# One attention layer on one core: the last step's seven products in another order, two weight sums made a step ahead

## The chip, the core and the metric

The kernel runs on one core of a Trainium2 chip. The metric is the device time of one execution in microseconds (us). A core has TensorE (PE; its weight loads are listed apart as PEld), VectorE (DVE), ScalarE (ACT), GpSimd (POOL) and SyncE (SP), which here issues nearly all DMAs. Each engine works through its own instructions in the order in which they are written into its queue.

## The reference

One layer of neighbourhood attention over a grid of 8 x 64 tokens, 16 heads of 128, D = 2048, all in float32:

```python
h = rms_norm(x, norm_pre)                      # x: 512 x 2048
q, k, v, z = split(h @ w_in, 4)                # w_in: 2048 x 8192
o = neighbourhood_attention(q, k, v, rpb)      # all 8 rows, 16 of the 64 columns
y = (o * silu(z)) @ w_out                      # w_out: 2048 x 2048
return x + rms_norm(y, norm_post)
```

## The kernel before

The program runs through ten steps. Step 0 to 7 compute h @ w_in, 1024 columns each (two heads' q, k, v and z); their attention runs beside the next step. Steps 8 (NSTEP) and 9 (LAST) compute the output product with w_out, 1024 columns each.

Every matmul is in a rounded format, so a float32 product is made of three: an operand is split into hi (a CAST on ACT) and lo = operand - hi (a subtraction on DVE), and hi x hi, hi x lo and lo x hi are summed in PSUM. A weight tile is 128x512, 256 KB, loaded as `raw` (NRAW = 4 buffers, by SP) or into one of eight resident tiles `t0` to `t7` (T[k]). `prep(m)` splits the weight of slot m and stands AHEAD = 2 slots ahead of the slot's matmuls; `at_prep` says which raw load is issued behind which prep, at least six preps ahead. `hi`/`lo` are the split weights; `a{k}_{n}` are the split activations.

Steps 0 and 8 are plain: 32 slots of 12 matmuls (L285). The others multiply 2 x 2 blocks in seven products: `B11`, `B12`, `B21`, `B22` are the blocks of the step's weights, the passes P1 to P7 (p = 0 to 6 in the code) have 8 slots of 6 matmuls (L332) each, and some of them take a sum of blocks as weights: T[k] is loaded with B11, and DVE adds raw blocks to it at L240 (`t<-t,raw`), ahead of the split, or behind it at L255. The products are summed in three PSUM chains, `"XYXYZYZ"[p]`: u9X, u9Y, u9Z are those of step 9, two tiles each. `combine` takes a chain's tiles at the end of a pass (s1, s5, e, c11 are its results); where the next pass goes on in the same tiles, PE waits for that reading. In step 9 the order of passes is LATE, and P2, the last, has its weights as the split tiles `a{k}_2`/`a{k}_3`, made from raw504 to raw511 by `late_prep` beside the passes before; its two halves (s = 0, 1) are computed one after the other.

`finish(n, t)` takes quarter n (512 columns) of row block t of y: a Square with a sum on ACT (L655), the product with the post weight gpost on DVE (L656), and, when a row block has all its sums, the mean (L658 to L661) and the power on POOL (L662). `final` then multiplies, adds the block of x (`xres`; for t = 0 it lies in T) and stores the result (L668, L670). Beside the second half of step 8 DVE also turns o * silu(z) back and splits it into `a{k}_n`, with t0 to t7 and zm as scratch (L64 is the helper for work that is kept in the order of the program).

At the start, twelve warm-up matmuls run while x (blocks of 128x512, scaled by gcol on ACT and split) and the first raws arrive.

## Time and profile before

| | us |
|---|---|
| median of 3 runs (lowest, highest) | 895.38 (894.34, 895.58) |
| the profiled execution | 896.13 |
| its span, first to last instruction | 894.4 |
| PE busy | 877.7 (98%) |
| DVE busy | 733.8 (82%) |
| ACT busy | 560.7 (63%) |
| moved by DMA | 168.65 MB, mean 189 GB/s |

In the profile all times count from the span's start. A row "[1.43 <-DVE e L363]" says that the engine stood idle for 1.43 us before it and that a DVE instruction of line 363, which writes e, ended that. "x4" is a group of instructions without a pause worth a row.

### The profile page before, as it was taken

The numbers are of one execution on the slowest core, as the hardware profiler recorded it, in microseconds if no ns is written. First come the engines' busy times: TensorE is split into PE (matmuls) and PEld (weight loads), VectorE is DVE, ScalarE is ACT, GpSimd is POOL, SyncE is SP. The second block draws the span as 40 slices with busy tenths as digits, with TensorE's granted clock in tenths as the row PEclk, the third lists the DMA queues.
The fourth block names the chain that finished last, engine by engine and source line by source line (L and its number), as shares of the span: only waits on it lengthen the run. The fifth ranks groups of instructions, "written<-read, shape, count | busy, mean of one in ns | idle before, by whom it ended". The sixth has DMA issues, their size and how long they took to land. (4 is left out here: it accounts for less than half of the span.)

```text
span 894.4 us, 13143 instructions
## 1 busy us (share of the span) xinstructions
PE 877.7 (98%) x4184; PEld 729.3 (82%) x4184; DVE 733.8 (82%) x1367; ACT 560.7 (63%) x1093; POOL 21.0 (2%) x42
## 2 busy tenths in 40 slices
PE   9999999999999999999999999999999999999995
PEld 8888888888888888888888888888888788888774
DVE  4567979897988898889878987998799845979987
ACT  7666857585758565856675667566766755555451
POOL 0000000000000000000000000000010100000000
PEclk9999999999999999999999999999999999999998
DMA  8768357646763765377547654774486534447877
GB/s 267 210 178 257 97 173 237 204 121 184 234 192 109 223 216 178 115 224 226 167 121 226 210 174 124 235 211 149 147 271 218 157 100 139 141 141 226 269 231 239
DMA packets 88277, 168.65 MB, mean 189 GB/s; under 512 B 10128, under 2 KB 10128, under 8 KB 88208
## 3 DMA queue, kind: packets, MB, share of 16 engines
q1 hardware_dynamic: 85536, 159.95, 59.4%
...
q10 hardware_dynamic: 432, 0.53, 0.2%
q14 instruction: 37, 0.30, 0.1%
...
## 5 line engine op out<-in xcount | busy, mean ns | idle before, releaser
L247 ACT CAST hi<-t 128x512 fp32r<-128x512 f32 x320 | 196.6, 618 | 132.2 <-DVE lo L248 21.5
L248 DVE TENSOR_TENSOR lo<-t,hi 128x512 fp32r<-128x512 f32 x320 | 217.3, 686 | 33.5 <-ACT hi L247 32.7
L248 DVE TENSOR_TENSOR lo<-raw,hi 128x512 fp32r<-128x512 f32 x184 | 125.9, 688 | 68.6 <-ACT hi L247 46.9
L247 ACT CAST hi<-raw 128x512 fp32r<-128x512 f32 x184 | 113.8, 620 | 99.2 <-PE u L285 24.7
L240 DVE TENSOR_TENSOR t<-t,raw 128x512 f32<-128x512 f32 x200 | 134.0, 686 | 7.5 <-DMA raw<-in_w 6.6
L285 PE MATMUL u<-hi,a 128*128 128x512 f32 x512 | 130.9, 392 | 1.4 <-DVE e L380 1.2
L285 PEld LDWEIGHTS u<-hi,a 128*128 128x128 f32 x512 | 94.9, 188 | 21.5 <-DVE e L380 1.8
L285 PE MATMUL u<-lo,a 128*128 128x512 f32 x256 | 70.8, 389 | 0.0
L285 PEld LDWEIGHTS u<-lo,a 128*128 128x128 f32 x256 | 48.0, 188 | 10.0
L255 DVE TENSOR_TENSOR t<-t,raw 128x512 f32<-128x512 f32 x56 | 37.3, 686 | 7.3 <-DMA raw<-in_w 7.3
L332 PE MATMUL u9Y<-hi,a 128*128 128x512 f32 x96 | 26.6, 393 | 0.5 <-ACT hi L247 0.5
L332 PE MATMUL u1Y<-hi,a 128*128 128x512 f32 x96 | 26.8, 396 | 0.0
L332 PE MATMUL u2Y<-hi,a 128*128 128x512 f32 x96 | 26.8, 396 | 0.0
L332 PE MATMUL u4Y<-hi,a 128*128 128x512 f32 x96 | 26.8, 396 | 0.0
L332 PE MATMUL u3Y<-hi,a 128*128 128x512 f32 x96 | 26.8, 396 | 0.0
L332 PE MATMUL u5Y<-hi,a 128*128 128x512 f32 x96 | 26.8, 396 | 0.0
L332 PE MATMUL u7Y<-hi,a 128*128 128x512 f32 x96 | 26.8, 396 | 0.0
L332 PE MATMUL u6Y<-hi,a 128*128 128x512 f32 x96 | 26.8, 396 | 0.0
L332 PEld LDWEIGHTS u9Y<-hi,a 128*128 128x128 f32 x96 | 17.8, 188 | 5.4 <-ACT hi L247 1.4
L545 POOL DMA_DIRECT2D graw<-zm x14 | 7.8, 554 | 561.7 <-DVE zm L539 561.7
L495 ACT ACTIVATE edge<-edge,nm 128x192 f32<-128x192 f32 x32 | 14.5, 455 | 8.7 <-DVE nm L488 8.7
L332 PEld LDWEIGHTS u4Y<-hi,a 128*128 128x128 f32 x96 | 17.4, 188 | 3.2
...
## 6 DMA issues: line engine op xcount, KB each, us to landing
raw<-in_w SPq DMA_DIRECT2D x392, 256.0 KB, 3.0
t<-in_w SPq DMA_DIRECT2D x128, 256.0 KB, 3.0
...
x<-in_xT SPq DMA_DIRECT2D x16, 256.0 KB, 3.9
graw<-zm POOLq DMA_DIRECT2D x14, 256.0 KB, 3.4
...
xres<-in_x SPq DMA_DIRECT2D x12, 256.0 KB, 4.1
out<-xres SPq DMA_DIRECT2D x10, 256.0 KB, 3.0
```

The source lines that it names most:

```text
L240: nc.vector.tensor_tensor(T[k], T[k], src, ALU.add)
L247: nc.scalar.copy(hi, src)
L248: nc.vector.tensor_tensor(lo, src, hi.bitcast(F32), ALU.subtract)
L255: nc.vector.tensor_tensor(T[k], T[k], src, ALU.add)
L285: nc.tensor.matmul(U[n][j], l, r, start=k == 0 and i == 0, stop=k == KT - 1 and i == 2)
L332: nc.tensor.matmul(U[c][s], l, r, start=p in (0, 1, 4) and k == 0 and n == 0, stop=k == KH - 1 and n == 2, skip_group_check=True,)
L495: nc.scalar.activation(p, p, AF.Exp, bias=nm[:, i : i + 1], accum_out=sm[:, i : i + 1])
L545: nc.gpsimd.dma_start(graw[h], z_of[h])
```

## The change

LATE becomes P7, P1, P5, P6, P4, P3, P2. P7's weights are B12 + B22: `t<-B12` is now loaded in the second half of step 8 (instead of B11), and DVE adds raw B22 (raw520 to raw527) to it there. P5's are B11 + B12: in the first half of step 8, B12 is loaded into `zw` tiles, raw B11 (raw512 to raw519) is added, the sum is stored to `wsum` in DRAM, and read back into T while P1 runs. P1's B11 is loaded into T while P7 runs. In LAST the chain Z starts at P7, X at P1 (on the PSUM tiles with tag T) and Y at P5; `combine_last` takes the results in the new order. The late activations lie in `a{k}_3` and N2/N3. In the plain step's second half (n = 1) the product with gpost is put off to slots 1 to 7 of LAST. xres is loaded from slot 16 on, every third slot, and finish of key "22" (quarter 3) comes eight slots sooner. At the start raw0 and raw1 are issued by ACT, ACT's table load follows them, hi0 is cast on DVE, and the first four blocks of x are scaled and split in the order of the program. Small tiles (rc, rcy, ms, msy; mx, sm, nm, rs) become slices of one tile.

```diff
-LATE = (0, 1, 3, 4, 6, 5, 2)
+LATE = (6, 0, 1, 3, 4, 5, 2)
...
+    def load_z(k):
+        Z[k] = cp.tile([P, L], F32, tag="zw", name=f"zw{k}", bufs=2)
+        nc.sync.dma_start(Z[k], w[LAST, B12, k])
+
+    def keep_z(k):
+        nc.sync.dma_start(wsum[k], Z.pop(k))
...
-        return step in PLAIN or p not in (0, 6) or step == LAST and p == 6
+        return step in PLAIN or p not in ((0, 1, 6) if step == LAST else (0, 6))
...
+    def sum_prep(m):
+
+        m -= base(NSTEP)
+        return [N + i * KH + (m - c) // 2 for i, c in ((0, 6), (1, 22)) if m in range(c, c + 2 * KH, 2)]
...
-        nc.sync.dma_start(raws[m], src)
+        (nc.scalar if m < 2 else nc.sync).dma_start(raws[m], src)
...
     def prep(m):
+        if m >= N:
+            i, k = divmod(m - N, KH)
+            t = T[k] if i else Z[k]
+            nc.vector.tensor_tensor(t, t, raws.pop(m), ALU.add)
...
-        if not plain and (p in (1, 3, 4) or step == LAST and p == 6):
+        if not plain and p in (1, 3, 4) and (step, p) != (LAST, 1):
...
-            hi, lo = (A(k, o).rearrange("p a b -> p (a b)") for o in (N2, A22))
+            hi, lo = (A(k, o).rearrange("p a b -> p (a b)") for o in (N2, N3))
...
-        nc.scalar.copy(hi, src)
+        if m == 0:
+
+            nc.vector.tensor_copy(hi, src)
+        else:
+            (act if m < 4 else nc.scalar).copy(hi, src)
...
-        elif p == 4:
+        elif p == 4 and step < LAST:
             load_t(step, B12, k)
...
-        elif p == 6 and step + 1 < NSTEP:
-            load_t(step + 1, B11, k)
+        elif p == 6 and (step + 1 < NSTEP or step == LAST):
+            load_t(min(step + 1, LAST), B11, k)
+        elif p == 0 and step == LAST:
+            nc.sync.dma_start(T[k], wsum[k])
...
+    def begins(step, p):
+        return p in (0, 1, 6 if step == LAST else 4)
...
-            if step == LAST and c == "Z":
+            if step == LAST and c == "X":
                 U[c] = [px.tile([P, L], F32, tag="T", name=f"u{step}{c}{s}") for s in range(2)]
...
+    def combine_last(c, u, p):
+
+        if p == 6:
+            c["22"] = pair("s7")
+            for s in range(2):
+                nc.scalar.copy(c["22"][:, s, :], u[s])
+        elif p == 0:
+            c["12"], c["11"] = pair("s1"), pair("c11")
+            for s in range(2):
+                nc.scalar.copy(c["12"][:, s, :], u[s])
+                nc.vector.tensor_tensor(c["22"][:, s, :], u[s], c["22"][:, s, :], ALU.add)
+        elif p == 1:
+            c["21"] = pair("s5")
+            for s in range(2):
+                nc.vector.tensor_tensor(c["21"][:, s, :], u[s], c["12"][:, s, :], ALU.add)
+        else:
+            for key in {3: ("22", "21"), 4: ("21",), 5: ("12",)}[p]:
+                for s in range(2):
+                    nc.vector.tensor_tensor(c[key][:, s, :], u[s], c[key][:, s, :], ALU.subtract)
...
+        if n == 1:
+
+            at(base(LAST) + 1 + 2 * (t ^ 2), lambda: nc.vector.tensor_tensor(y, src, gb[n], ALU.mult))
+            return
         nc.vector.tensor_tensor(y, src, gb[n], ALU.mult)
...
+    for k in range(KH):
+        at(base(NSTEP) + 1 + 2 * k, load_z, k)
+        at(base(NSTEP) + 5 + 2 * k, keep_z, k)
...
-        at(base(LAST) + (KH + 7 * i // 2 if i < KH else 4 * KH + 4 + 2 * q), load_res, t, q)
+        at(base(LAST) + (2 * KH + 3 * i if i < KH else 4 * KH + 4 + 2 * q), load_res, t, q)
...
-            at(base(LAST) + 5 * KH + 1 + 2 * s, lambda n=n, key=key, s=s: finish(n, 2 + s, C[LAST][key][:, s, :]))
+            at(base(LAST) + (7 - n) * KH + 1 + 2 * s, lambda n=n, key=key, s=s: finish(n, 2 + s, C[LAST][key][:, s, :]))
```

What it moves is seen best in the engines' queues. DVE at the end of step 8, before (lo456 is the first weight of LAST; L64 are the rotations and splits, L240 the adds for P5, L656 the products with gpost):

```order
L248 TENSOR_TENSOR lo456_8393<-t0_142,hi456_8392 128x512
L64 TENSOR_TENSOR a7_3_141<-t7_149,a7_3_141 128x2x256
L240 TENSOR_TENSOR t0_142<-t0_142,raw464_8445 128x512
L248 TENSOR_TENSOR lo457_8412<-t1_143,hi457_8411 128x512
L240 TENSOR_TENSOR t1_143<-t1_143,raw465_8459 128x512
L656 TENSOR_TENSOR y1_0_8418<-u8_1_0_8087,gpost0_7953 128x512
L656 TENSOR_TENSOR y1_1_8424<-u8_1_1_8088,gpost0_7953 128x512
L656 TENSOR_TENSOR y1_2_8430<-u8_1_2_8089,gpost0_7953 128x512
```

And now, from three rows behind the split of `a6_3`, the last reader of t6 as scratch (L281 is the split of a weight, L259 the new adds, L65 the helper, L712 the product with gpost):

```order
L65 TENSOR_TENSOR zm15_7816<-t7_147,zm15_7816 128x256
L65 TENSOR_TENSOR t7_147<-t7_147 128x256
L259 TENSOR_TENSOR t6_146<-t6_146,raw526_8369 128x512
L65 TENSOR_TENSOR t7_147<-t7_147,zm15_7816 128x256
L281 TENSOR_TENSOR lo456_8409<-t0_140,hi456_8408 128x512
L65 TENSOR_TENSOR zm15_7816<-zm15_7816,t7_147 128x256
L65 TENSOR_TENSOR a7_3_139<-t7_147,a7_3_139 128x2x256
L281 TENSOR_TENSOR lo457_8432<-t1_141,hi457_8431 128x512
L712 TENSOR_TENSOR y1_0_8439<-u8_1_0_8079,gpost0_7930 128x512
L259 TENSOR_TENSOR t7_147<-t7_147,raw527_8414 128x512
L712 TENSOR_TENSOR y1_1_8444<-u8_1_1_8080,gpost0_7930 128x512
L281 TENSOR_TENSOR lo458_8459<-t2_142,hi458_8458 128x512
```

The adds for P5 are gone; those for P7 stand between the splits, the ones of t6 and t7 a few rows behind the rows that last read these tiles as scratch, and the products with gpost are parted.

DVE where a chain goes over from one pass to the next, before (L363 reads Z between P4 and P7):

```order
L248 TENSOR_TENSOR lo488_8861<-t0_142,hi488_8860 128x512
L248 TENSOR_TENSOR a1_2_116<-raw505_8877,a1_3_117 128x512
L248 TENSOR_TENSOR lo489_8874<-t1_143,hi489_8873 128x512
L363 TENSOR_TENSOR e_9_8765<-u9Z0_8777,e_9_8765 128x512
L363 TENSOR_TENSOR e_9_8765<-u9Z1_8778,e_9_8765 128x512
L248 TENSOR_TENSOR lo490_8893<-t2_144,hi490_8892 128x512
```

And now, between P5 and P6 (L432 reads Y for s5, L269 adds to T):

```order
L281 TENSOR_TENSOR lo481_8742<-t1_141,hi481_8741 128x512
L432 TENSOR_TENSOR s5_8753<-u9Y0_8657,s1_8645 128x512
L432 TENSOR_TENSOR s5_8753<-u9Y1_8658,s1_8645 128x512
L281 TENSOR_TENSOR lo482_8758<-t2_142,hi482_8757 128x512
L269 TENSOR_TENSOR t1_141<-t1_141,raw489_8802 128x512
L269 TENSOR_TENSOR t2_142<-t2_142,raw490_8830 128x512
```

and between P6 and P4 (L436 reads Y for s7 and s5):

```order
L281 TENSOR_TENSOR lo489_8853<-t1_141,hi489_8852 128x512
L436 TENSOR_TENSOR s7_8553<-u9Y0_8657,s7_8553 128x512
L436 TENSOR_TENSOR s7_8553<-u9Y1_8658,s7_8553 128x512
L436 TENSOR_TENSOR s5_8753<-u9Y0_8657,s5_8753 128x512
L436 TENSOR_TENSOR s5_8753<-u9Y1_8658,s5_8753 128x512
L281 TENSOR_TENSOR lo490_8876<-t2_142,hi490_8875 128x512
L281 TENSOR_TENSOR lo491_8889<-t3_143,hi491_8888 128x512
```

The reading that a next pass waits for has moved from Z to Y, and four subtractions stand in one place.

PE at the end of the last pass but one, before (raw503 is its last weight; 36 matmuls of X follow its last row):

```order
L332 MATMUL u9Y0_8547<-hi503_9112,a7_1_139 128x512 x2
L332 MATMUL u9Y1_8548<-hi503_9112,a7_1_139 128x512 x2
L332 MATMUL u9X0_8447<-a3_2_124 128x512
L332 MATMUL u9Y0_8547<-lo503_9113,a7_1_139 128x512
L332 MATMUL u9Y1_8548<-lo503_9113,a7_1_139 128x512
```

And now (44 matmuls of X follow the last row of Y; two are shown):

```order
L370 MATMUL u9Y0_8657<-hi503_9094,a7_1_137 128x512 x2
L370 MATMUL u9Y1_8658<-hi503_9094,a7_1_137 128x512
L370 MATMUL u9Y0_8657<-lo503_9095,a7_1_137 128x512
L370 MATMUL u9Y1_8658<-hi503_9094,a7_1_137 128x512
L370 MATMUL u9Y1_8658<-lo503_9095,a7_1_137 128x512
L370 MATMUL u9X0_8562<-a1_3_115,a1_2_114 128x512 x2
```

Fewer matmuls of X stand among those of Y, and more behind them.

## Rows read from the trace of the kernel before

**Rows 1.** The page: the span, each engine's busy time, its share of the span and its instructions, and the granted clock in 40 slices, in tenths of full speed (9 is 90% or more).

```profile
span 894.4 us, 13143 instructions
PE 877.7 (98%) x4184; PEld 729.3 (82%) x4184; DVE 733.8 (82%) x1367; ACT 560.7 (63%) x1093; POOL 21.0 (2%) x42
...
PEclk9999999999999999999999999999999999999998
```

**Rows 2.** What PE waited for in the whole span: us in total, times, longest.

```profile
PE u9Z L332 <- DVE e L363: 1.4, 1, 1.4
PE u9Y L332 <- DVE lo L248: 1.3, 2, 1.0
...
PE u9Y L332 <- ACT hi L247: 0.5, 1, 0.5
```

**Rows 3.** The timeline of PE and ACT in LAST: start, us, engine, line, operation, out<-in, count, and idle time before with what ended it. 802.58 is LAST's first matmul, 874.17 the first one on raw503, 873.50 the cast of raw503.

```profile
802.58 1.07 PE L332 MATMUL u9X<-hi,a 128*128 128x512 f32 x4
...
849.07 1.10 PE L332 MATMUL u9Z<-hi,a 128*128 128x512 f32 x3 [1.43 <-DVE e L363]
...
874.17 1.20 PE L332 MATMUL u9Y<-hi,a 128*128 128x512 f32 x4
...
873.50 0.62 ACT L247 CAST hi<-raw 128x512 fp32r<-128x512 f32 x1 [1.29 <-DMA raw<-in_w]
```

**Rows 4.** The chain of work that ended last, in order of time: start, us, what. The first two lie in step 8, the others in LAST.

```profile
715.83 0.47 PE s L463 x4
...
756.29 46.45 PE u L285 x204
...
840.99 3.78 DMA raw<-in_w
...
846.13 6.01 DMA raw<-in_w
```

**Rows 5.** Stretches: bounds and length, busy time of each engine, the granted clock, the mean DMA share and GB/s. The first is step 8's first half, the second its second half.

```profile
705.00:757.00 52.00, 51.18 (x266) 42.82 (x266) 29.61 (x67) 29.79 (x65) 1.08 (x2) 1.00 0.44 124
757.00:803.00 46.00, 46.00 (x203) 37.92 (x203) 37.77 (x74) 23.66 (x47) 0.00 (x0) 1.00 0.47 138
...
845.00:860.00 15.00, 13.57 (x59) 10.54 (x57) 11.74 (x19) 6.34 (x11) 0.00 (x0) 1.00 0.85 259
...
867.00:878.00 11.00, 10.22 (x43) 7.46 (x42) 10.17 (x21) 4.35 (x9) 2.09 (x2) 1.00 1.03 317
```

**Rows 6.** DMA issues by line, count, KB each, median us from issue to landing: the first row in step 8 (705 to 803), the others in LAST (801 to 876).

```profile
t<-in_w SPq DMA_DIRECT2D x8, 256.0 KB, 2.7
...
raw<-in_w SPq DMA_DIRECT2D x43, 256.0 KB, 3.4
xres<-in_x SPq DMA_DIRECT2D x12, 256.0 KB, 4.1
t<-in_w SPq DMA_DIRECT2D x8, 256.0 KB, 4.1
t<-in_x SPq DMA_DIRECT2D x4, 256.0 KB, 4.9
```

**Rows 7.** The timeline of the start, all engines: the issue of raw0, hi0, lo0 and the first matmuls of the layer.

```profile
1.18 0.42 SPq L229 DMA_DIRECT2D raw<-in_w  x1
...
5.30 0.61 ACT L247 CAST hi<-raw 128x512 fp32r<-128x512 f32 x1
...
5.95 0.69 DVE L248 TENSOR_TENSOR lo<-raw,hi 128x512 fp32r<-128x512 f32 x1
...
5.97 2.11 PE L285 MATMUL u<-hi,a 128*128 128x512 f32 x8 [0.20 <-ACT hi L247]
```

**Rows 8.** The timeline of the end, all engines: the finals of row block 0, the last matmul, and the last Square, its sum and the product behind it.

```profile
883.23 1.42 DVE L668 SCALAR_TENSOR_TENSOR t<-y,rcy,t 128x512 f32<-128x512 f32 x2 [0.65 <-POOL rcy L662]
...
883.83 0.39 PE L332 MATMUL u9X<-a 128*128 128x512 f32 x1
...
884.32 0.58 ACT L655 ACTIVATE ysq<-u9X 128x512 f32<-128x512 f32 x1 [4.75 <-PE u9X L332]
...
884.81 0.19 ACT L655 ACTIVATION_READ_ACCUMULATOR ysq<-u9X 128x1 f32 x1
...
885.89 0.69 DVE L656 TENSOR_TENSOR c<-u9X,gpost 128x512 f32<-128x512 f32 x1
```

**Rows 9.** The timeline of DVE in step 8, 709 to 715 (first half) and 783 to 804 (second half).

```profile
709.24 0.69 DVE L248 TENSOR_TENSOR lo<-raw,hi 128x512 fp32r<-128x512 f32 x1 [0.67 <-ACT hi L247]
...
713.09 0.69 DVE L248 TENSOR_TENSOR lo<-raw,hi 128x512 fp32r<-128x512 f32 x1 [1.28 <-ACT hi L247]
...
714.69 0.68 DVE L418 SCALAR_TENSOR_TENSOR q14l<-tq,q14h 128x512 fp32r<-128x512 f32 x1
...
783.79 0.69 DVE L248 TENSOR_TENSOR lo<-raw,hi 128x512 fp32r<-128x512 f32 x1 [1.22 <-ACT hi L247]
...
785.46 0.43 DVE L64 TENSOR_TENSOR t<-t 128x256 f32<-128x256 f32 x1
...
801.46 2.05 DVE L656 TENSOR_TENSOR y<-u,gpost 128x512 f32<-128x512 f32 x3
803.42 0.68 DVE L248 TENSOR_TENSOR lo<-t,hi 128x512 fp32r<-128x512 f32 x1
```

**Rows 10.** DVE in LAST: one row of the timeline, and the group of the adds in 803 to 876 (count, busy us, mean ns, idle us before and what ended most of it).

```profile
848.33 1.28 DVE L363 TENSOR_TENSOR e<-u9Z,e 128x512 f32<-128x512 f32 x2
...
L240 DVE TENSOR_TENSOR t<-t,raw 128x512 f32<-128x512 f32 x30 | 20.4, 689 | 2.1 <-DMA raw<-in_w 1.7
```

More of the change, by code (lines that the diff above doesn't have):

```diff
@@ L103, in na_block @@
         nc.gpsimd.memset(edge[i][:, zero], 0.0)
-    rc = cp.tile([P, 4], F32, name="rc")
+    rows = cp.tile([P, 16], F32, name="rows")
+    rc, rcy, ms, msy = (rows[:, i : i + 4] for i in range(0, 16, 4))
     part = cp.tile([P, 4, 4], F32, name="part")
-    ms = cp.tile([P, 4], F32, name="ms")
     AT = {}
@@ L124, in load_t @@
         (sync if step == 1 and q == B11 else nc.sync).dma_start(T[k], w[step, q, k])
+    Z = {}
+    wsum = dp.tile([KH, P, L], F32, name="wsum")
+    def load_z(k):
[3 more added lines that the diff above has]
+        nc.sync.dma_start(wsum[k], Z.pop(k))
     X = {}
@@ L157, in take_x @@
     def take_x(k):
-        nc.scalar.activation(X[k], X[k], AF.Copy, scale=gcol[:, k : k + 1])
-        take(k)
+        scalar = act if k < 4 else nc.scalar
+        scalar.activation(X[k], X[k], AF.Copy, scale=gcol[:, k : k + 1])
+        take(k, scalar)
     def sum_x(k):
@@ L211, in late_prep @@
         return [N - KH + i] if 0 <= i < KH and not odd else []
+    def sum_prep(m):
+        m -= base(NSTEP)
+        return [N + i * KH + (m - c) // 2 for i, c in ((0, 6), (1, 22)) if m in range(c, c + 2 * KH, 2)]
     raws, at_prep = {}, {}
-    preps = [j for m in range(N - KH) for j in [m] + late_prep(m)]
+    preps = [j for m in range(N - KH) for j in [m] + late_prep(m) + sum_prep(m)]
     place = {m: i for i, m in enumerate(preps)}
-    seq = [m for m in preps if is_raw(m)]
+    seq = [m for m in preps if m >= N or is_raw(m)]
     for i, m in enumerate(seq):
@@ L223, in load_raw @@
         raws[m] = wp.tile([P, L], F32, tag="raw", name=f"raw{m}", bufs=NRAW)
+        if m >= N:
+            i, k = divmod(m - N, KH)
+            nc.sync.dma_start(raws[m], w[LAST, (B11, B22)[i], k])
+            return
         step, p, k = where(m)
@@ L228, in load_raw @@
             src = w[step, (None, B12, B21, B22, B21, B22, B22)[p], k]
-        nc.sync.dma_start(raws[m], src)
+        (nc.scalar if m < 2 else nc.sync).dma_start(raws[m], src)
     W = {}
     def prep(m):
+        if m >= N:
+            i, k = divmod(m - N, KH)
+            t = T[k] if i else Z[k]
+            nc.vector.tensor_tensor(t, t, raws.pop(m), ALU.add)
+            for r in at_prep.get(m, ()):
+                load_raw(r)
+            return
         step, p, k = where(m)
@@ L302, in mm_seven @@
         c = chain(p)
-        if p in (0, 1, 4) and k == 0:
+        if begins(step, p) and k == 0:
             b = (step + (c == "Y")) % 2
-            if step == LAST and c == "Z":
+            if step == LAST and c == "X":
                 U[c] = [px.tile([P, L], F32, tag="T", name=f"u{step}{c}{s}") for s in range(2)]
@@ L335, in products @@
                 r,
-                start=p in (0, 1, 4) and k == 0 and n == 0,
+                start=begins(step, p) and k == 0 and n == 0,
                 stop=k == KH - 1 and n == 2,
@@ L343, in combine @@
         c = C.setdefault(step, {})
-        if p == 0:
+        if step == LAST:
+            combine_last(c, u, p)
+        elif p == 0:
             c["12"] = pair(f"s1_{step}")
@@ L367, in combine @@
             for s in range(2):
-                if step == LAST:
-                    finish(3, s, c["12"][:, s, :])
-                else:
-                    scale_c(c["12"], s, 0)
-        elif step == LAST:
-            c["11"] = pair(f"c11_{step}")
-            for s in range(2):
-                nc.vector.tensor_tensor(c["21"][:, s, :], u[s], c["21"][:, s, :], ALU.subtract)
-                nc.vector.tensor_tensor(c["22"][:, s, :], c["22"][:, s, :], u[s], ALU.subtract)
+                scale_c(c["12"], s, 0)
         else:
@@ L384, in combine @@
                 scale_c(c["22"], s, 2)
+    def combine_last(c, u, p):
[3 more added lines that the diff above has]
+                nc.scalar.copy(c["22"][:, s, :], u[s])
+        elif p == 0:
+            c["12"], c["11"] = pair("s1"), pair("c11")
[10 more added lines that the diff above has]
+                    nc.vector.tensor_tensor(c[key][:, s, :], u[s], c[key][:, s, :], ALU.subtract)
+            if p == 5:
+                for s in range(2):
+                    finish(3, s, c["12"][:, s, :])
     def scale_c(t, s, j):
@@ L469, in add_bias @@
         if a == 0:
-            col_of[h] = [sp.tile([P, 4], F32, tag=t, name=f"{t}{h}") for t in ("mx", "sm", "nm", "rs")]
+            col = sp.tile([P, 16], F32, tag="col", name=f"col{h}")
+            col_of[h] = [col[:, i : i + 4] for i in range(0, 16, 4)]
         mx, _, nm, _ = col_of[h]
@@ L632, in na_block @@
             if step:
-                at(base(step) + KT + 2 * k, load_t, LAST, B11, k)
+                at(base(step) + KT + 2 * k, load_t, LAST, B12, k)
             at(base(step) + KT + 1 + 2 * k, lambda k=k: split_a(k, X[k + KH], N4, act, dve))
-    ms3 = cp.tile([P, 4], F32, name="ms3")
-    msy = cp.tile([P, 4], F32, name="msy")
-    rcy = cp.tile([P, 4], F32, name="rcy")
+    ms3 = ms
     yg, xres, gb = {}, {}, {}
@@ L701, in na_block @@
             prep(m + AHEAD)
-            for j in late_prep(m + AHEAD):
+            for j in late_prep(m + AHEAD) + sum_prep(m + AHEAD):
                 prep(j)
```

11 lines of the change are left out of this document (6 added, 5 removed).

## The prediction

> **What bounds the kernel now.** I read the engines' shares first: PE is busy in 98% of the span, DVE in 82%, ACT in 63%, and the granted clock of TensorE is full in every slice but the last [rows 1]. So the time is PE's matmuls one after the other, and a gain can come from three places: the time before the first matmul, PE's stalls, and what follows the last matmul. The list of what PE waited for is short: 1.4 us at u9Z for DVE's L363 and 1.3 + 0.5 us at u9Y for weights (lo, hi) are most of it [rows 2]. All three lie in LAST, the step that the change rewrites.
>
> How much LAST loses is seen from its two ends. Its first matmul starts at 802.58 and its last ends at 883.83 + 0.39 = 884.22 [rows 3, 8]: 81.6 us. It has 56 slots of 6 matmuls; undisturbed, 204 matmuls of step 8 take 46.45 us [rows 4], 0.228 each, so a slot is 1.37 us and LAST without stalls is 76.5 us. About 5 us are lost: 1.43 of waiting before 849.07, where the Z chain starts anew and waits for DVE, and weights that come late up to 874.17 [rows 3].
>
> The second loss is transfers. In the chain of work that ended last, PE gives way to raw loads: 3.78 us of DMA from 840.99, 6.01 from 846.13 [rows 4]. By stage, the DMA share is 0.44 to 0.47 in step 8 (124 to 138 GB/s) and 0.85 in LAST's middle (259 GB/s), 1.03 (317 GB/s) at its fullest [rows 5]. A t load lands 2.7 us after its issue in step 8, loads in LAST after 3.4 to 4.9 us [rows 6]. The last weight (raw503) is ready for ACT only at 873.50, after 1.29 us of waiting for DMA [rows 3]; the matmuls that use it start at 874.17, and the 10.05 us to 884.22 hold little but its slot (1.37) and 36 matmuls of X (8.2). So that load sets the end of PE's work.
>
> **The change part by part.** Number of matmuls and their shapes are unchanged, so PE's 877.7 us stay.
>
> *Start.* Before, ACT casts hi0 at 5.30 (0.61 us) though raw0 was issued at 1.18; first matmul 5.97 [rows 7]. Now raw0 and raw1 are issued on ACT's queue, in turn with x0, x1 on SP's, and DVE casts hi0 first of all. When raw0 lands I have no row for. If as early as now, it is there before 5.30, and a DVE pass over a 128x512 tile (0.69 us for lo [rows 7]; the cast itself has no row) from about 4.4 gives 5.1; if it shares with x1 it comes a load later, 256 KB at the 317 GB/s of a full stretch [rows 5] = 0.83 us, then hi0 is ready at 5.9, as now. DVE must then do lo0 and the a splits behind it, which slot 0's later matmuls need. Gain between 0.6 and -0.3; I take **-0.3 us**. The Trainium skill, "DMA: Bandwidth & Descriptors", section "Issuing engines are not separate DMA queues", says that DMAs started by different engines run on the same 16 DMA engines and interleave, and that only sequencer time is saved. The trace before has nothing but a small load on ACT's queue there, so no row decides it; by that rule raw0 shares with x1 and this term is 0 or above, by a landing as early as now it is -0.6.
>
> *Step 8, first half: eight adds into zw (L259, 0.69 us each the mean of L240 [rows 10]), 8 + 8 loads and 8 stores.* DVE is busy 29.6 of 52.0 us there [rows 5], so 5.5 us fit. The one with a price stands between lo428 and lo429, ahead of k14l and q14l, which PE's scores need at 715.83 [rows 4] against a q14l that ends at 714.69 + 0.68 [rows 9]: 0.5 us of slack, and raw512, issued when DVE has freed a raw buffer with the lo at 709.24 + 0.69 [rows 9], lands at 712.6 if it takes the 2.7 us of t [rows 6], or 1 us later. lo429 starts at 713.09 before [rows 9], so it and all behind it move back by 0.2 to 1.2 us. Loss 0 to 0.6 us; **+0.2**. On SP the store of each sum waits for its add, and the next raws stand behind it; they are issued six preps ahead, over ten us in this step, so I cost it at nothing; uncovered, it is the add's own wait, 0.7 us a time.
>
> *Step 8, second half: eight adds T = B12 + B22.* DVE has 1.22 us idle (before 783.79 [rows 9]), and so again in each two slots of 12 matmuls, 5.46 us. Two adds in a row take 1.28 (two L363 [rows 10]), 0.6 more than one, so one or two fit. The adds for t0 to t5 fit. t6 and t7 are scratch of the rotation up to the splits a6_3 and a7_3 and are loaded only then. Between split and add stand four rows for t6 (two of 0.6 us, two half tiles of 0.43 [rows 9]: 2.1) and two for t7 (1.2), against a load of 2.7 us [rows 6]: DVE waits 0.6 and 1.5 us. Behind both is lo458. Before, it starts at 803.42 and ends at 804.1 [rows 9]; P7's third slot begins at 802.58 + 2 x 1.37 = 805.3 and uses lo after four matmuls, at 806.2, so it has 2.1 us of slack. Now it comes later by 2.1 of waits and 1.2 of adds, earlier by one mult (0.6) and by what idle time is left (0.6): 2.1 us, just at its slack. Loss 0 to 1.2 us; **+0.35**. In exchange the y<-u,gpost mults (three in 2.05 us [rows 9]) are spread over the first slots, and LAST's first pass needs neither raw loads nor adds.
>
> *LAST's transfers.* Before, 43 raws, 8 t and 16 blocks of x (12 xres, 4 t<-in_x) are loaded from 801 on, 67 [rows 6]. Now the diff leaves 32 raws (480 to 511, three of them issued sooner), 8 t, 8 sums read back from DRAM and the 16 of x, some 61; the t and the sums come in the first 16 slots, where no raw is used. Step 8 takes 24 loads and 8 stores, 8.4 MB over 98 us = 86 GB/s on top of its 124 to 138: under the 259 of LAST [rows 5], so hidden there.
>
> *LAST's hand-offs.* Z now starts in the first pass and X on its own PSUM tiles, so the 1.43 us wait at 849.07 has no cause left. P5 to P6 is a hand-off within Y: PE waits for s5<-u9Y, two DVE reads behind lo481. Two such reads took 1.28 (L363 [rows 10]), the second PSUM half hidden behind the first: 0.6 to 0.9 us. Four subtractions at the next change of pass (L436, 4 x 0.6 = 2.4 us back to back) stand ahead of lo490 and lo491; AHEAD is two slots = 2.7 us: 0 to 1 us.
>
> *LAST's end.* With NRAW = 4 each raw load waits for the DVE or ACT work on the raw four before. The last 24 raws (488 to 511) with their xres and t come as densely as before, at 1.01 us per load by 259 GB/s or 0.83 by 317 [rows 5]. Followed along SP's order from P6's start, raw503 lands 67.4 to 69.1 us after LAST's start (an estimate from these two spacings); before, 873.50 - 802.58 = 70.9. But 44 matmuls of X are left after it (10.0 us) where there were 36 (8.2). With 0.7 us from ACT's start to the first matmul (873.50 to 874.17 [rows 3]) and 1.37 for its slot, LAST is 67.4 to 69.1 + 12.1 = 79.5 to 81.2 us, against 81.6. Stalls of the hand-offs fall into this wait. Bounds: +0.5 (nothing won, one hand-off on top) to -4.3 (5 us less 0.7 for Y's hand-off, if no load binds). I take **-1.6 us**, inside the estimate's gain of 0.4 to 2.1 and past its middle, since the Z hand-off's 1.4 us, which held back DVE and so the raw buffers, is gone.
>
> *Tail.* The last half of X: Square ends at 884.32 + 0.58, its sum at 884.81 + 0.19 = 885.00, but DVE does four finals of t from 883.23 and comes to c<-u9X only at 885.89 [rows 8]; the power on POOL, four finals and the stores follow it. These t finals start late because c's first half stood behind all four finals of row block 3; in the new queue two of these stand ahead of s1<-u9Y instead, and with 1.42 us for two finals [rows 8] all behind them comes up to 1.4 us sooner. Then c waits only for the Square and its sum: 885.89 - 885.00 = 0.9 us, up to 1.4 if the finals at the end gain too. **-1.0 us**; 0 if DVE is as late as before.
>
> Sum: -0.3 + 0.2 + 0.35 - 1.6 - 1.0 = **-2.35 us**. The profiled execution took 896.13 (span 894.4, 1.7 around it); the median of the runs is 895.38. So 895.4 - 2.35 = **893.0 us** for the median.
>
> **The rivals.**
> (A) The sum as above, 891.3 to 894.6. Chance 0.45.
> (B) No load binds in LAST any more. For: 67 to 61 loads, and the eight adds with the worst waits (L240 waits 1.7 us for DMA [rows 10]) are spread. Against: 24 raws at the end are as dense as before. Then LAST gains 4.3: -0.3 + 0.55 - 4.3 - 1.0 = -5.05, 890.3. Chance 0.22.
> (C) The change does not do what it says: raw503 lands as late as before, the stalls only move. Then -0.3 + 0.55 + 0 - 1.0 = -0.75: 894.6. For: NRAW, the bandwidth and the late pass are the same. Chance 0.20.
> (D) Slower, by one mechanism: DVE's queue stands behind an add whose operand is still loading. t6 and t7 (and the zw adds) wait at the head of DVE's queue; if a load there takes the 4.1 to 4.9 us of LAST [rows 6] instead of 2.7, since t, raws and the read-back meet at 795 to 805, the two waits grow by 1.8 us each, 3.6 together past lo458's slack. With C's end of LAST and the zw adds' 0.6 that is -1.3 + 0.6 + 3.6 = +2.9, 898.3. It decides from 2.5 us of such stalls on, where LAST's end gives nothing back. For: the order of rows; against: step 8's DMA share of 0.47. Chance 0.13.
>
> **How the numbers follow.** A measurement of this kernel tells from no change about 0.2%, 1.8 us: faster is below 893.6, slower above 897.2. Of A two thirds lie below 893.6 (0.30), the rest is the same (0.15); B is faster (0.22); C the same (0.18, and 0.02 below); D slower in 0.10, the same in 0.03. So faster 0.54, same 0.36, slower 0.10. The range 889.8 to 896.4 leaves out the lower half of B (0.1) and most of D (0.1); A's own is 891.3 to 894.6.
>
> **What would show it.** In the changed profile: first matmul at 5.2 to 5.9; no PE wait at u9Z; a wait of 0.6 to 0.9 us at u9Y for L432; PE waits in step 8's last or LAST's first three slots for lo, and an L259 row with "<-DMA t"; raw503's hi 68 to 70 us after LAST's start, still with a wait for DMA; c<-u9X right behind the last Square. The prediction is wrong low if PE waits at P7 for more than 1.2 us or raw503 is as late as before, and wrong high if the passes P4 and P3 show no PE wait at all.

## The result: slower by 0.37%

The changed kernel takes 898.57 us (median of 18 runs) against 895.25 for the kernel before: ratio 1.0037, 95% interval 1.0023 to 1.0051. A second series gave 1.0018 (1.0008 to 1.0028). It is slower, by 1.6 to 3.3 us, where 2.35 us less was forecast; the time lies above the range.

The profiled execution took 897.59 us (span 895.8), 1.46 more than that of before. Stage by stage:

| us | before | after |
|---|---|---|
| first matmul of the layer at | 5.97 | 5.68 |
| second matmul of step 8 at | 705.82 | 704.89 |
| from there to LAST's first matmul | 96.76 | 98.20 |
| LAST, first to last matmul | 81.64 | 83.31 |
| last matmul to the end of the span | 10.18 | 9.39 |

The start and the tail gained 0.29 and 0.79 us, near the 0.3 and 1.0 forecast; step 8 and LAST lost 1.44 and 1.67 us where a gain of 1.05 was forecast for both together. Between the first two rows lies a gain of 0.64 us that was not forecast; there the traces of kernels with the same steps differ by up to 2. Two executions of kernels further down (one of e4 with 3149 us, one of e5 with 4643) ran slow and stand in no figure. What PE waited for in the changed kernel (whole span; us in total, times, longest):

```profile
PE u9Z L370 <- DVE lo L281: 1.8, 1, 1.8
PE u9Y L370 <- ACT hi L280: 1.4, 2, 0.9
...
PE u9Y L370 <- DVE s L432: 0.7, 1, 0.7
...
PE o L589 <- DVE pt_1l L479: 0.5, 1, 0.5
PE tz L466 <- DVE k14l L479: 0.4, 1, 0.4
```

Against [rows 2], the wait of 1.4 us at u9Z for e (the Z chain's start) is gone as forecast, and another of 1.8 us at u9Z, for a lo, has come: P7 starves in its third slot. The last two lie in step 8's first half, where [rows 2] has nothing.

DVE's timeline there tells why (start, us, ..., idle time before and what ended it):

```profile
797.69 0.69 DVE L281 TENSOR_TENSOR lo<-raw,hi 128x512 fp32r<-128x512 f32 x1
...
801.49 0.69 DVE L259 TENSOR_TENSOR t<-t,raw 128x512 f32<-128x512 f32 x1 [1.72 <-DMA t<-in_w]
...
804.58 0.68 DVE L712 TENSOR_TENSOR y<-u,gpost 128x512 f32<-128x512 f32 x1
807.02 0.69 DVE L259 TENSOR_TENSOR t<-t,raw 128x512 f32<-128x512 f32 x1 [1.76 <-issue]
...
808.23 0.68 DVE L281 TENSOR_TENSOR lo<-t,hi 128x512 fp32r<-128x512 f32 x1
```

The two adds of t6 and t7 stand at the head of DVE's queue for 1.72 and 1.76 us, and lo458 behind them starts at 808.23, where it started at 803.42 [rows 9]. The row at 797.69 is lo455; before, DVE did it at 794.67.

```profile
806.00 1.20 PE L370 MATMUL u9Z<-hi,a 128*128 128x512 f32 x4
808.96 0.74 PE L370 MATMUL u9Z<-lo,a 128*128 128x512 f32 x2 [1.77 <-DVE lo L281]
```

At the end of LAST, SP's issues of raws (start, us; the next row starts when SP may go on):

```profile
848.27 2.22 SPq L251 DMA_DIRECT2D raw<-in_w  x3
850.54 0.54 SPq L65 DMA_DIRECT2D xres<-in_x  x1
858.45 0.97 SPq L251 DMA_DIRECT2D raw<-in_w  x2
```

SP stands for 7.4 us, from 851.08 to 858.45. The load it holds is raw508; its buffer is raw495's, and that one's add comes on DVE only at 857.75, behind the four L436 and the two products of quarter 3. In this time the channel is half empty, and what is left then comes in one burst (stretches; the last two figures are DMA share and GB/s):

```profile
845.00:860.00 15.00, 15.00 (x68) 12.41 (x67) 14.69 (x29) 8.82 (x18) 0.00 (x0) 1.00 0.55 168
...
867.00:878.00 11.00, 9.34 (x37) 6.50 (x37) 9.61 (x16) 4.17 (x8) 0.98 (x1) 1.00 1.05 291
```

Against 0.85 and 1.03 in [rows 5], the middle of LAST is emptier and the end as full as before. raw503 is cast at 874.04, 70.95 us after LAST's first matmul at 803.09; before it was 70.92 [rows 3]:

```profile
874.04 0.62 ACT L280 CAST hi<-raw 128x512 fp32r<-128x512 f32 x1 [1.36 <-DMA raw<-in_w]
```

The tail: c's product now follows the last Square at once, where [rows 8] has it behind four finals.

```profile
886.51 0.58 ACT L709 ACTIVATE ysq<-u9X 128x512 f32<-128x512 f32 x1 [4.75 <-PE u9X L370]
887.00 0.20 ACT L709 ACTIVATION_READ_ACCUMULATOR ysq<-u9X 128x1 f32 x1
887.23 0.69 DVE L714 TENSOR_TENSOR c<-u9X,gpost 128x512 f32<-128x512 f32 x1 [1.24 <-ACT ysq L709]
```

The 1.46 us of the two profiled executions are less than the 3.3 us of the medians. The changed kernel's 18 runs spread from 895.4 to 902.4, those of before from 893.4 to 897.9; the mean granted clock tells the two ends apart: the five runs at 0.997 or 0.998 took 895.4 to 897.0, the six at 0.994 or 0.995 took 898.7 to 902.0; the seven at 0.996 lie between and above, 897.6 to 902.4.

### The profile page after: what moved, and what is told of

Its sections match the earlier page's. It is cut to its first block, busy times and chain, and to the rows that moved or that the text cites. A ratio compares the mean times of both kernels' runs of the same rounds, so it can differ in the third digit from the quotient of the medians.

```text
span 895.8 us, 13172 instructions
## 1 busy us (share of the span) xinstructions
PE 878.9 (98%) x4184; PEld 729.3 (81%) x4184; DVE 733.6 (82%) x1369; ACT 560.1 (63%) x1092; POOL 20.9 (2%) x42
## 3 DMA queue, kind: packets, MB, share of 16 engines
q10 hardware_dynamic: 720, 1.06, 0.4%
## 5 line engine op out<-in xcount | busy, mean ns | idle before, releaser
L281 DVE TENSOR_TENSOR lo<-t,hi 128x512 fp32r<-128x512 f32 x320 | 217.6, 685 | 40.3 <-ACT hi L280 39.3
L281 DVE TENSOR_TENSOR lo<-raw,hi 128x512 fp32r<-128x512 f32 x184 | 125.9, 688 | 53.9 <-ACT hi L280 41.0
L280 ACT CAST hi<-raw 128x512 fp32r<-128x512 f32 x180 | 111.4, 620 | 88.1 <-PE u L323 22.2
L269 DVE TENSOR_TENSOR t<-t,raw 128x512 f32<-128x512 f32 x184 | 122.8, 684 | 4.8 <-DMA raw<-in_w 4.2
L288 DVE TENSOR_TENSOR t<-t,raw 128x512 f32<-128x512 f32 x56 | 37.2, 685 | 4.3 <-DMA raw<-in_w 4.2
L551 ACT ACTIVATE edge<-edge,col 128x192 f32<-128x192 f32 x32 | 14.5, 454 | 9.0 <-DVE col L544 9.0
L370 PEld LDWEIGHTS u2Y<-hi,a 128*128 128x128 f32 x96 | 17.4, 188 | 3.2
```

The lines of the kernel that those rows point to most:

```text
L269: nc.vector.tensor_tensor(T[k], T[k], src, ALU.add)
L280: (act if m < 4 else nc.scalar).copy(hi, src)
L281: nc.vector.tensor_tensor(lo, src, hi.bitcast(F32), ALU.subtract)
L288: nc.vector.tensor_tensor(T[k], T[k], src, ALU.add)
L370: nc.tensor.matmul(U[c][s], l, r, start=begins(step, p) and k == 0 and n == 0, stop=k == KH - 1 and n == 2, skip_group_check=True,)
L551: nc.scalar.activation(p, p, AF.Exp, bias=nm[:, i : i + 1], accum_out=sm[:, i : i + 1])
```

## The experiments

My theory after the result: two rows stand late at the head of DVE's queue (the adds of t6 and t7, and the add of raw495), and both places starve PE. The rivals: the transfers that the change adds, or moves together, are what is late (bandwidth); or one of the two sums is itself the loss, wherever its adds stand. Each run was timed against the kernel before on its own chip (e0 to e3 on one, e4 to e7 on a second, e8 to e10 on a third), so I compare the ratios; 0.001 is 0.9 us, and by the intervals a difference of two of the ratios is uncertain by 0.0014 to 0.0019, 1.3 to 1.7 us. In the code the products P1, P5, P2, P6, P4, P3, P7 are p = 0 to 6, in this order.

| kernel | ratio to before | 95% interval |
|---|---|---|
| changed, second series (e0) | 1.0018 | 1.0008 to 1.0028 |
| t6, t7 added later (e1) | 0.9989 | 0.9979 to 0.9998 |
| finish of quarter 3 as late as before (e2) | 1.0013 | 1.0003 to 1.0022 |
| before, with the new start (e3) | 1.0001 | 0.9990 to 1.0013 |
| no sum through DRAM (e4) | 1.0009 | 0.9996 to 1.0022 |
| own buffers for raw504 to raw511 (e5) | 1.0028 | 1.0012 to 1.0043 |
| e1 and e5 together (e6) | 0.9978 | 0.9967 to 0.9990 |
| P7's sum in the last step (e7) | 0.9998 | 0.9987 to 1.0009 |
| e6 with PE held in P7, four adds (e8) | 1.0016 | 1.0002 to 1.0031 |
| the same, seven adds (e9) | 1.0039 | 1.0025 to 1.0052 |
| e6 without the sum through DRAM (e10) | 0.9963 | 0.9950 to 0.9977 |

**e0, the changed kernel again.** No edit.

> The changed kernel once more, for a second trace and its spread on this chip. If the loss sits in fixed places (queue heads): again 2.5 to 4 us slower than before, PE stalls again in P7's third and fourth slot (1 to 4 us for lo) and at the end of LAST (2 to 3 us), and the spread of its times, wider than that of before, shows as a different size of these same stalls. If the loss is elsewhere (the first trace was only 1.5 us longer than before's): stalls at other places than these.

Measured: +1.6 us, less than the 2.5 to 4 that I expected. The stalls of its trace lie where they lay: 2.03 + 0.14 us in P7, 0.70 at Y's hand-off, 1.12 and 0.77 at the end of LAST; one of 0.34 in step 8's first half. So the places are fixed, and the size varies.

**e1, the adds of t6 and t7 later.**

```diff
-        return [N + i * KH + (m - c) // 2 for i, c in ((0, 6), (1, 22)) if m in range(c, c + 2 * KH, 2)]
+        if m in (FIRST + 5, FIRST + 6):
+            return [N + KH + m - FIRST + 1]
+        return [N + i * KH + (m - c) // 2 for i, c in ((0, 6), (1, 22)) if m in range(c, c + 2 * (KH - 2 * i), 2)]
...
-            nc.vector.tensor_tensor(t, t, raws.pop(m), ALU.add)
+            (dve if m >= N + KH + 6 else nc.vector).tensor_tensor(t, t, raws.pop(m), ALU.add)
```

> The adds of t6 and t7 come three slots later in DVE's queue, behind lo461 and lo462. If the head of DVE's queue is what is lost at P7 (add waiting for its t load, lo458 behind it): the stall at P7 falls from 2.2 us to under 0.4, and the time by 1.5 to 2.3 us against the changed kernel. If the loads themselves are late (bandwidth): the stall moves to P7's last two slots and the time stays within 0.5 us.

Measured: 0.0029 less than e0, 2.6 us. In its trace P7 runs without a stall:

```profile
805.41 0.62 PE L372 MATMUL u9Z<-lo,a 128*128 128x512 f32 x2
805.87 1.07 PE L372 MATMUL u9Z<-hi,a 128*128 128x512 f32 x4
806.77 0.39 PE L372 MATMUL u9Z<-lo,a 128*128 128x512 f32 x1
```

This is the slot that broke off for 1.77 us in the changed kernel. The loads are the same in number and size, so it was the place of the two adds in the queue and not the bandwidth. The end of LAST still stalls (1.14 and 1.10 us).

**e2, the finish of quarter 3 as late as before.** In this kernel the mean square of row blocks 2 and 3 is taken before quarter 3's part is in; the instructions are the same in number and kind.

```diff
-            at(base(LAST) + (7 - n) * KH + 1 + 2 * s, lambda ...
+            at(base(LAST) + 5 * KH + 1 + 2 * s, lambda ...
```

> One part undone: finish of quarter 3 of row blocks 2 and 3 comes as late as before, so the add of raw495 stands eight rows sooner in DVE's queue. If raw508 and the raws behind it are late because that add, which frees raw495's buffer, is stuck in DVE's queue (SP stands from 850.5 to 858.5): raw508 is issued 2 to 4 us sooner, the stalls at the end of LAST fall from 2.6 to under 1.5 us and the time by 1 to 2 us. If bandwidth sets raw503's landing: it lands as before against LAST's start, and the time stays within 0.5 us.

Measured: 1.0013, not to be told from e0. raw508 is issued at 857.08, 54.6 us after LAST's start against 55.4 in the first trace. That is only 0.7 us sooner because PE lost more time in P7 here. Against P4's first matmul it is 5.3 us instead of 8.0, and SP stands for 4.5 us instead of 7.4: the edit freed the buffer 2.7 us sooner, and the end stalls are as long (1.56 and 0.59, in sum 2.2 against 1.7 and 2.1). So this one buffer is not what holds up the end of LAST, and that half of my theory fails. What its trace shows instead is the granted clock (the column before DMA share) behind P7's stall, here 2.15 us:

```profile
808.00:809.00 1.00, 0.28 (x1) 0.28 (x2) 1.00 (x3) 0.24 (x1) 0.00 (x0) 1.00 0.46 88
...
810.00:811.00 1.00, 1.00 (x3) 0.47 (x2) 1.00 (x3) 0.35 (x1) 0.00 (x0) 0.50 0.73 223
811.00:812.00 1.00, 1.00 (x4) 0.71 (x4) 1.00 (x3) 0.27 (x1) 0.00 (x0) 0.50 0.32 80
812.00:813.00 1.00, 1.00 (x4) 0.81 (x3) 0.88 (x2) 0.00 (x0) 0.00 (x0) 0.50 0.99 377
```

0.50 is 1.2 GHz instead of 2.4: for some 3.4 us matmuls start 0.43 us apart instead of 0.227, which costs 1.5 us on top of the stall.

**e3, the kernel before with the new start alone** (the table load and x's order as in the change, too).

```diff
...
-        nc.sync.dma_start(raws[m], src)
+        (nc.scalar if m < 2 else nc.sync).dma_start(raws[m], src)
...
-        nc.scalar.copy(hi, src)
+        if m == 0:
+            nc.vector.tensor_copy(hi, src)
+        else:
+            (act if m < 4 else nc.scalar).copy(hi, src)
...
```

> The kernel before with the start of the changed one (raw0, raw1 on ACT's queue, hi0 on DVE, table load behind them). If the start is worth what the two traces show: 0.3 us faster than before, slot 1 at 8.5 to 8.6 against 8.82. If the later x blocks (x4 and on) pay it back: 0.0, with waits at other slots of step 0.

Measured: 1.0001; 0.1 us more, give or take 1. Its trace has the first matmul at 5.66 and slot 1 at 8.61, sooner by 0.31 and 0.21 than before, much as in the changed kernel. A gain of that size can't be told from none by these runs.

**e4, no sum through DRAM.** P5's raw B12 is loaded and added in LAST as before.

```diff
-        return step in PLAIN or p not in ((0, 1, 6) if step == LAST else (0, 6))
+        return step in PLAIN or p not in (0, 6)
...
-        if not plain and p in (1, 3, 4) and (step, p) != (LAST, 1):
+        if not plain and p in (1, 3, 4):
...
-    for k in range(KH):
-        at(base(NSTEP) + 1 + 2 * k, load_z, k)
-        at(base(NSTEP) + 5 + 2 * k, keep_z, k)
```

> One part undone: P5's sum is made in the last step again (raw B12 loaded and added while P5 is prepared), nothing goes through DRAM and step 8's first half has no adds and 24 transfers less. If queue heads are what is lost (P7's t6 and t7 are unchanged): the 0.6 us stalls in step 8's first half go, the stall at P7 stays at 2 us, and P5 gets waits for raws; in sum within 1 us of the changed kernel. If the added traffic of step 8 is what delays t6's load (3.6 us to landing): the stall at P7 falls by half and the time by 1 us or more.

Measured: 1.0009, 0.8 us less than e0, which the intervals do not part. Step 8's first half has no stall in the trace; P7's falls to 0.23 + 0.13 us though its adds stand in the same places and wait as long:

```profile
798.81 0.69 DVE L259 TENSOR_TENSOR t<-t,raw 128x512 f32<-128x512 f32 x1 [1.77 <-DMA t<-in_w]
...
804.20 0.69 DVE L259 TENSOR_TENSOR t<-t,raw 128x512 f32<-128x512 f32 x1 [1.62 <-issue]
...
805.41 0.68 DVE L281 TENSOR_TENSOR lo<-t,hi 128x512 fp32r<-128x512 f32 x1
```

All of it comes 2.7 to 2.8 us sooner than in the changed kernel, with PE only 1 us ahead of it. So the waits are not longer by the added traffic (t6's load lands in 3.7 us here and 3.6 there), but DVE's lead over PE, which has to cover them, is shorter in the changed kernel: step 8's raws and adds for the other sum had used it up (the rows stand in the part on why the prediction was wrong). Both of my readings had a part.

**e5, own buffers for raw504 to raw511**, the two zw tiles.

```diff
-    for i, m in enumerate(seq):
-        e = max(place[m] - 6, place[seq[i - NRAW]] if i >= NRAW else 0)
-        if i > 2:
-            at_prep.setdefault(preps[e], []).append(m)
+    lates = range(N - KH, N)
+    for own, depth in (([m for m in seq if m not in lates], NRAW), (list(lates), 2)):
+        for i, m in enumerate(own):
+            e = max(place[m] - 6, place[own[i - depth]] if i >= depth else 0)
+            if i > 2 or m in lates:
+                at_prep.setdefault(preps[e], []).append(m)
...
+        if m in lates:
+            raws[m] = cp.tile([P, L], F32, tag="zw", name=f"raw{m}", bufs=2)
...
```

> raw504 to raw511 (P2's weights) get the two zw buffers, free by then, so they no longer take turns with the four raw buffers of P4 and P3. If buffers held by adds late in DVE's queue set the end of the last step: SP no longer stands 7 us before raw508, raw503's cast comes 1.5 to 3 us sooner against the step's start (70.95 before), end stalls 2.6 to under 1.2 us, time 1 to 2 us less than the changed kernel; the stall at P7 stays. If bandwidth sets it (DMA share 1.02 there): within 0.5 us.

Measured: 1.0028, not less than e0 but 0.9 us more, within the intervals. The end did become better: its waits are 0.6 us in sum instead of 1.7 and 2.1 in the two traces of the changed kernel, and raw503 is cast 69.46 us after LAST's start though P7's stall is longer here. SP still stands, from 852.94 to 860.09, but fewer loads are left behind it (8 raws instead of 10). So more buffers help the end, though the stand that I had blamed is as long as before. In this trace the time went to P7: 2.45 us of stall, and behind it the clock:

```profile
808.00:810.00 2.00, 0.00 (x0) 0.00 (x0) 1.95 (x4) 0.43 (x1) 0.00 (x0) 1.00 0.02 5
810.00:812.00 2.00, 2.00 (x5) 1.61 (x6) 2.00 (x4) 0.62 (x1) 0.00 (x0) 0.57 0.75 240
812.00:814.00 2.00, 2.00 (x7) 1.52 (x6) 1.89 (x4) 0.62 (x1) 0.00 (x0) 0.57 0.65 195
```

**e6, both mends**, the diffs of e1 and e5 together.

> The later adds of t6 and t7 and the two own buffers for raw504 to raw511 together. If both causes are right and independent: 3 to 4 us less than the changed kernel, 893 to 894, which is 1.5 to 2.5 us under the kernel before, with P7 and the end of the last step nearly without stalls. If the end is set by bandwidth: as with the later adds alone, 895.2.

Measured: 0.9978, 3.6 us less than e0 and 2.0 less than before. In LAST two waits are left:

```profile
PE u9Y L377 <- DVE s L439: 0.8, 1, 0.8
PE u9Y L377 <- ACT hi L287: 0.5, 1, 0.5
```

LAST takes 78.46 us in this trace, 3.2 less than before, and raw503 is cast 64.98 us after its start. Its 12 runs have a clock of 0.996 or 0.997. Against e1, which mends P7 alone, it is 1.0 us less, and e5, which adds the buffers alone, was 0.9 us more than e0: the intervals part neither from nothing. In the traces the buffers show: the waits at the end of LAST are 0.51 us in sum instead of e1's 2.45, and LAST takes 78.46 us instead of 81.25.

**e7, P7's sum in the last step**, so that t6's add stands ahead of lo458 and t7's behind it.

```diff
...
-        return [N + i * KH + (m - c) // 2 for i, c in ((0, 6), (1, 22)) if m in range(c, c + 2 * KH, 2)]
+        return [N + i * KH + (m - c) // 2 for i, c in ((0, 6),) if m in range(c, c + 2 * KH, 2)]
...
-        if not plain and p in (1, 3, 4) and (step, p) != (LAST, 1):
+        if not plain and (p in (1, 3, 4) and (step, p) != (LAST, 1) or (step, p) == (LAST, 6)):
```

> One part undone: P7's sum is made in the last step (raw B22 added while P7 is prepared); t0 to t7 are still loaded with B12 in step 8. t6's add still stands ahead of lo458 in DVE's queue, t7's two splits behind it. If the head of DVE's queue is what is lost: the stall at P7 is smaller than 2.2 us by t7's part (1.5), 0.5 to 1.2 us are left, time 1 to 1.7 us less than the changed kernel. If making the sum a step ahead is itself what costs (DVE time in step 8): step 8's stalls go too. If it is what helps: P7 waits for raws, and the time is longer.

Measured: 0.9998, 1.8 us less than e0. P7 has no stall, where I expected 0.5 to 1.2 us to be left; in step 8's first half one of 0.19 us stays. So it is again the place of the adds, and not only of t7's: made by the last step's own rule those of t0 to t5 stand later too, and DVE has its lead back before t6's comes. P7 doesn't wait for its raws.

**e8 and e9, PE held in P7.** To price a stall by itself: e6, and four or seven adds into an unused tile on DVE ahead of lo458.

```diff
+        if m == base(LAST) + 2:
+            spare = cp.tile([P, L], F32, tag="zw", name="spare", bufs=2)
+            for _ in range(4):
+                dve.tensor_tensor(spare, src, src, ALU.add)
...
```

> To measure what a stall of PE in P7 costs by itself: the kernel with both mends (later adds of t6 and t7, own buffers for raw504 to raw511), in which P7 has no stall, plus four adds into an unused tile on DVE just ahead of lo458. lo458 then comes 3.6 us later (4 x 0.6, and two rows of 0.6 that now stand ahead of it), 1.8 us past its slack. If a stall costs its own length: 1.8 us more than with both mends, 895.1, and the granted clock stays full. If the granted clock falls behind the stall, as in two of five traces with stalls of 2.15 and 2.45 us (0.5 for some 3.5 us), the time grows by up to 1.7 us more, to 896.8, and the runs spread.

> The same with seven adds: a stall of 3.6 us in P7. If a stall costs its own length: 3.6 us more than with both mends, 896.9. If the granted clock falls behind a stall of this length every time: a stretch at 0.5 in the trace and 1.5 to 2 us on top, 898.5 to 899.

Measured: 3.4 and 5.5 us more than e6 for stalls of 2.28 and 4.56 us. In both traces the clock falls around the end of the stall; e9's:

```profile
808.00:810.00 2.00, 0.00 (x0) 0.00 (x0) 1.90 (x4) 0.00 (x0) 0.00 (x0) 1.00 0.00 0
810.00:812.00 2.00, 1.05 (x3) 0.91 (x4) 2.00 (x4) 0.62 (x1) 0.00 (x0) 0.82 0.19 70
812.00:814.00 2.00, 2.00 (x6) 1.51 (x6) 1.31 (x3) 0.30 (x1) 0.00 (x0) 0.50 1.00 353
814.00:816.00 2.00, 2.00 (x9) 1.59 (x8) 1.29 (x2) 0.34 (x2) 0.00 (x0) 0.83 0.86 298
```

In these traces LAST is longer than e6's by the stall and 1.5 to 1.6 us more (82.38 and 84.57 us against 78.46), which is the clock; the medians give 1.1 and 0.9 us beyond the stall, with the 1.7 us of uncertainty named above. All seven runs of e9 have a mean clock of 0.993 to 0.995, where of the 19 runs of the kernel before on that chip three have 0.995 and none less; so it may well fall in all of them. Of e8's twelve runs four have 0.992 to 0.995 (898.2 to 899.5 us) and eight 0.996 to 0.998 (894.1 to 898.4): there it seems to fall in some, but the mean clock of a run does not say where it fell. The spread of the changed kernel's first series did not come again: e8's runs lie within 5.4 us and e9's within 3.1, those of the kernel before on that chip within 4.9.

**e10, both mends and no sum through DRAM**, the diffs of e6 and e4 together.

> Both mends, and P5's sum made in the last step again (no sums through DRAM). If the sum through DRAM is worth its 24 transfers in step 8: 0.5 to 1.5 us slower than with both mends, with waits of P5 for raws. If it costs more in step 8 (two stalls of 0.6 us in its first half) than it gives: 0.5 to 1.2 us faster.

Measured: 0.9963 (0.9950 to 0.9977), 3.3 us less than before and the best of all; against e6 1.3 us less, which the intervals do not part. Step 8 has no stall of over 0.1 us between its second matmul and its end; the hand-off in LAST is longer, 1.4 us where e6 has 0.8:

```profile
PE u9Y L375 <- DVE s L437: 1.4, 1, 1.4
PE u9Y L375 <- ACT hi L287: 0.9, 1, 0.9
```

Whether the sum through DRAM costs more in step 8 than it gives in LAST is not shown: by the runs it does, by the two traces step 8 is 0.42 us shorter without it (96.86 against 97.28, from its second matmul to LAST's first) and LAST 1.06 longer (79.52 against 78.46). What is shown is that the rest of the change is worth 3 us against the kernel before once two adds are moved and eight raws have buffers of their own.

## Why the prediction was wrong

*Start.* -0.3 forecast; slot 0 of the changed kernel begins 0.29 us sooner in the trace, and by e3 the time can't tell it from nothing. raw0 on ACT's queue landed at about 5.0 (hi0 waits for it), between my two bounds; before, it had landed at 4.4. (The early bound comes to 0.8 us by its own figures, 5.9 to 5.1, and not to 0.6.)

```profile
5.06 0.43 DVE L278 CAST hi<-raw 128x512 fp32r<-128x512 f32 x1 [4.05 <-DMA raw<-in_w]
```

The trace agrees there with the Trainium skill, "DMA: Bandwidth & Descriptors", section "Issuing engines are not separate DMA queues": a second queue did not bring raw0 sooner. What made up for it is that hi0 no longer stands behind ACT's work on x0, which had kept it waiting for 0.9 us after raw0's landing, and that DVE's cast took 0.43 us, less than the 0.69 that I took from the lo.

*Step 8, first half.* +0.2 forecast (0 to 0.6); PE stands for 0.36 us behind k14h as described, and for 0.46 at pt_1l, which I had not looked at. From step 8's second matmul to LAST's first the changed kernel lost 1.44 us in its first trace and 0.72 in its second; e4 and e10, which have no such adds, lost 0.1. The term was mis-sized: I priced one add of eight.

*Step 8: the step that failed.* It is the sentence on the raws of these adds, "they are issued six preps ahead, over ten us in this step, so I cost it at nothing". Seven of the eight adds into zw waited for their raw at the head of DVE's queue, 1.2 to 2.7 us each and 12.1 in all, where I had named 0.7 us a time for the worst. The first and the last:

```profile
712.46 0.69 DVE L259 TENSOR_TENSOR zw<-zw,raw 128x512 f32<-128x512 f32 x1 [1.64 <-DMA raw<-in_w]
...
761.64 0.69 DVE L259 TENSOR_TENSOR zw<-zw,raw 128x512 f32<-128x512 f32 x1 [2.74 <-DMA raw<-in_w]
```

The last one's raw was issued at 756.14 and landed 5.5 us later. PE hardly stood in these waits, so they looked free; what they used up is DVE's lead, the time from the end of a weight's lo to PE's first matmul on it. For lo455, the last ahead of t6's add, it is read from two rows each, of before, the changed kernel, e4 and e7 in turn:

```profile
794.67 0.69 DVE L248 TENSOR_TENSOR lo<-raw,hi 128x512 fp32r<-128x512 f32 x1 [1.23 <-ACT hi L247]
800.31 0.39 PE L285 MATMUL u<-lo,a 128*128 128x512 f32 x1
...
797.69 0.69 DVE L281 TENSOR_TENSOR lo<-raw,hi 128x512 fp32r<-128x512 f32 x1
800.83 0.39 PE L323 MATMUL u<-lo,a 128*128 128x512 f32 x1
...
794.95 0.69 DVE L281 TENSOR_TENSOR lo<-raw,hi 128x512 fp32r<-128x512 f32 x1
799.87 0.39 PE L321 MATMUL u<-lo,a 128*128 128x512 f32 x1
...
796.81 0.69 DVE L281 TENSOR_TENSOR lo<-raw,hi 128x512 fp32r<-128x512 f32 x1
802.16 0.39 PE L323 MATMUL u<-lo,a 128*128 128x512 f32 x1
```

The lead is 4.9 us before, 2.4 in the changed kernel (1.8 to 2.3 in e0, e2 and e5), 4.2 without the adds into zw (e4), and 4.7 with them but with P7's adds later (e7). So neither lot of adds takes it alone. The last add into zw cuts it: at lo442, the first weight behind it, the lead is 2.9 us before, 1.2 in the changed kernel and 1.1 in e7. The adds for t0 to t5 then fill the idle time in which DVE would gain it back, as it does in e7 by lo451 (6.3 us, as before; 3.5 in the changed kernel). "The adds for t0 to t5 fit" was right for these adds alone. I counted their time against the 1.22 us that DVE waits per two slots, and forgot what this waiting meant: DVE ran as far ahead of PE as the hi/lo buffers allow.

At P7 it comes due: +0.35 forecast (0 to 1.2), PE stood for 1.77 + 0.15 us, and for 2.0 to 2.4 in e0, e2 and e5. lo454 came 4.3 us later than before and lo455 3.0, ahead of t6's add, and DVE waited 1.72 and 1.76 us for t6 and t7 (the profile names the load for the first alone), where I had 0.6 and 1.5. The slack of 2.1 us at lo458 that I worked out from [rows 9] was no longer there. With nearly the whole lead the working holds: in e4 nearly the same two waits (1.77 and 1.62 us) leave PE a stall of 0.23 + 0.13, just at the slack. So it was the mechanism of rival D, given 0.13, that DVE's queue stands behind an add whose operand is still loading; its sizes were others. D reckoned with 4.1 to 4.9 us for the loads of t6 and t7, and t6's took 3.6; for all adds into zw it had 0.6, and their raws took 3.5 to 5.5 from issue to landing.

A stall of this length can have a price of its own, the clock, which no row of before could show, since its longest wait (1.43 us) left the clock full.

*Transfers.* Right in total (63 loads from 801 on against 67 before, 61 forecast), wrong in time: in 845 to 860 the DMA engines were busy for 0.55 of it, where I had reckoned with bandwidth.

*LAST's hand-offs.* Z's wait is gone and Y's is 0.70 to 0.74 us in the two traces, as forecast (0.6 to 0.9). The four L436 cost PE nothing directly. They put off the add of raw495, which stands behind them, and with it raw508's load; that this cost PE anything is not shown (e2).

*LAST's end.* -1.6 forecast, with raw503 67.4 to 69.1 us after the start; measured 70.95. The mark I named for rival C, raw503 as late as before, came, but by the stall in P7 and not for C's reason. Where P7 doesn't stall and the raw buffers are still four, raw503 is cast 68.86 (e1) and 68.30 us (e7) after LAST's start, inside the estimate, and LAST takes 81.25 and 80.65 us, against the 79.5 to 81.2 forecast. A stall in P7 puts raw503 off by its length: from e6 to e9 raw503 and the end of LAST both come 6.1 us later after LAST's start, 4.56 of stall and the rest of clock. So the loads go along with PE, through the buffers that its work frees, and not by a spacing of 0.83 to 1.01 us each. What is left of the miss is size: without the stall LAST gains 0.4 to 1.0 us, and nothing bore out taking 1.6, past the estimate's middle. That the raw buffers set the end is shown by the waits there, 0.1 to 0.9 us in sum in the five traces with own buffers (e5, e6, e8 to e10) and 1.7 to 2.4 in the six with four; which of them, stays open.

*Tail.* -1.0 forecast, -0.79 measured. Right, and for the reason given.

D's own reckoning, 898.3 from C's end with stalls in P7, is 0.3 us from the median of the first series. So close a figure is luck: PE stood for 1.9 us at P7 and not 3.6, raw503 was late by that stall and not for C's reason, and the second series lies 1.6 us above before and not 2.9.
